# A hybrid attention and conv-GLU layer on one core: first loads in another order and partly from ScalarE, and two output-projection tiles side by side

## Chip, cores and metric

One core of a Trainium2 chip runs the kernel. The metric is the device time of one execution in microseconds. Three runs of the kernel before gave 912.3, 916.3 and 916.69 us, median 916.3.

## What is computed

One layer over 16 meta tokens and 512 tokens of width 1024 (528 rows in all): three kinds of attention, gated and merged, an output projection, and a feed-forward part with a convolution of width 3. All of it is float32.

```python
u = rmsnorm(h, attn_norm)
z = u @ w_in                     # q, k, v of three branches, the indexer's q, k, w, three gates
y_sb = stick_breaking(...)       # 4 heads
y_sp = indexed_sparse(...)       # 4 heads, top 132 keys by the indexer's score, relative bias
y_df = differential(...)         # 4 heads with two softmaxes each, relative bias
merged = sum(sigmoid(g + b) * (y @ w_br))      # over the three branches
h = h + merged @ w_out
u = rmsnorm(h, ffn_norm)
gate, val = split(u @ w_up)
h = h + (silu(conv3(gate) + conv_b) * val) @ w_down
return h[16:528]
```

## The kernel before

Everything is held transposed: 128 channels on the partitions, tokens along the free dimension. The weights come as 133 chunks of 128 x 1024 float32 (512 KB each), every chunk the eight 128 x 128 tiles of one output tile. A product is made of three matmuls: both operands are split into a high part that TensorE takes in one pass and a low part, and the three products high-high, high-low and low-high are added up in PSUM (`mm3`, lines 311 to 324). So each chunk needs a cast on ACT (`wh`, line 306) and a subtraction (`wl`, line 307) that goes to DVE or POOL by booked costs (`sub`). There are three buffers for raw chunks, and two each for `wh` and `wl`. `order` (line 279) lists the chunks as they are used; `prep` loads two chunks ahead, from the SP queue.

An engine's instructions run in the order in which they were recorded. A layer of the kernel records them with a small model of the engines' clocks (`Timed`, `pe`, `tick`), and the tile framework may move an instruction by priority; what comes out is fixed before the kernel runs.

**The start (lines 339 to 415).** `prm` is a table of parameters, its first 40 columns are the gains. `hT` comes in eight k-tiles `hs[0..7]` (264 KB each, named `tmp<-hT`). Two chunks, W_IX (chunk 0) and W_QIX (chunk 1), are loaded in halves of four tiles (256 KB). Line 386 loops over the k-tiles: ACT scales one into `xh`, DVE makes `xl`, ACT squares it, and PE makes 12 matmuls, six for W_IX into `psw` and six for W_QIX into `psd`. After the last, DVE's sum of squares goes through a matmul with `onesd` (line 413), and `rstd` makes the reciprocal root on ACT and DVE; the results in PSUM are multiplied by it when they leave. Chunk 2 is W_QIX's second tile, chunks 3 and on are the attention units' q, k and v.

**The bias table.** `bias` (97 rows of 664 numbers) is loaded into `braw` by POOL at line 439. `bias_stream` (line 441) is a side stream: ACT casts parts of `braw` into two tiles `brd`, DVE makes a low part, and later a matmul and DMAs spread the table out. PE's matmul on `brd` comes at 39 us.

**The output projection (lines 1058 to 1099).** `mh` and `ml` are the split of the merged branches, eight k-tiles. Tile m uses chunk 59 + m: two halves of the tokens (258 and 256), 24 matmuls each, into one bank `psd` and one `psw` that `psx` hands out in turn. The first tile goes k-tile by k-tile in groups (0 to 3), (4, 5), (6), (7), since the last k-tiles of `mh` and `ml` come late. Then DVE adds the result to `hm`, ACT makes `uh` and the squares, DVE `ul`, POOL sums the squares.

In the profile nearly all work of DVE, ACT and POOL stands at line 99 (the helper that books it), and matmuls at line 183; so one goes by the tiles' names.

Of the kernel before, what the change touches and what calls it, by code (L numbers as in the profile page):

```python
# [15 lines left out]
P = 128  # L16
# [18 lines left out]
C_AN, C_FN, C_BG, C_QSP, C_KSP, C_QDF, C_KDF, C_SUB, C_CB, C_CW, C_LAM = (  # L35
    0, 8, 16, 40, 41, 42, 43, 44, 45, 67, 133)
# [3 lines left out]
W_IX, W_QIX, W_UNIT, W_GATE = 0, 1, 3, 27  # L40
# [15 lines left out]
def tile_kernel(ctx: ExitStack, tc, hT, wpk, par, bias, yT):  # L56
    nc = tc.nc
# [83 lines left out]
    def psd():  # L141
        return ps.tile([P, 512], F32, tag="d", bufs=banks["d"], name="psd")
# [36 lines left out]
    def mm(out, lhsT, rhs, **k):  # L179

        n, w = rhs.shape[-1], 0.84 * max(32, lhsT.shape[-1])
        pe(max(0.46 * n + 1, w) if rhs.dtype == F32R else 2 * max(0.844 * n, w))
        PE.matmul(out, lhsT, rhs, **k)  # L183
# [11 lines left out]
    def tick():  # L195
        for s in list(streams):
            cur[0] = s[1]
            try:
                next(s[0])
            except StopIteration:  # L200
                streams.remove(s)
        cur[0] = main
# [35 lines left out]
            n += 1  # L238
            assert n < 10000, (free, clock)

    nc.scalar.preload_act_table_set("natural_log_exp_and_others")


    prm = const.tile([P, NPAR], F32, name="prm")

    def pc(c):
        return prm[:, c:c + 1]
# [29 lines left out]
    wraw, wsp = {}, {}  # L277
    plan = PLAN.split()
    order = [W_IX, W_QIX, W_QIX + 1]
    for w in plan:  # L280
# [5 lines left out]
        else:  # L286
            n = BRW[br] // 2
# [5 lines left out]
    def load(k):  # L293
        if k is not None and k not in wraw:
            r = wp.tile([P, 8, P], F32, tag="raw", bufs=3, name=f"wr{k}")
            nc.sync.dma_start(r, wpk[k].rearrange("p (j c) -> p j c", c=P))
            wraw[k] = r

    def prep(k):
        if k is None or k in wsp:  # L300
            return
        load(k)
        r = wraw[k]
        wh = wp.tile([P, 8, P], F32R, tag="wh", bufs=2, name=f"wh{k}")
        wl = wp.tile([P, 8, P], F32R, tag="wl", bufs=2, name=f"wl{k}")
        S.copy(wh, r)
        sub(wl, r, wh, HVW)
        wsp[k] = (wh, wl)
        load(after.get(after.get(k)))

    def mm3(out, prs, xh, xl, start=True, stop=True):

        n = len(prs)
        c = 0
        for pas in range(3):
            for e, (k, j, kt) in enumerate(prs):
                wh, wl = wsp[k]
                w = wl if pas == 2 else wh
                x = xl if pas == 1 else xh
                mm(out, w[:, j, :], x(kt), start=start and pas == 0 and e == 0,  # L320
                   stop=stop and pas == 2 and e == n - 1)
                c += 1
                if c % 8 == 0:
                    tick()

    HALF = ((0, TH), (TH, TH))
    HALQ = ((0, HQ), (HQ, 256))
# [11 lines left out]
    def load_h(*kts):  # L339
        for kt in kts:  # L340
            nc.sync.dma_start(hs[kt], hT[:, kt])

    def load_half(k, a):
        nc.sync.dma_start(wraw[k][:, a:a + 4], wpk[k].rearrange("p (j c) -> p j c", c=P)[:, a:a + 4])


    nc.sync.dma_start(prm[:, :C_QSP], par[:, :C_QSP])
    load_h(0)
    load_half(W_IX, 0)
    load_half(W_QIX, 0)  # L350
    load_h(1, 2)
    load_half(W_IX, 4)
    load_h(3)
    load_half(W_QIX, 4)
    load_h(4, 5)
    nc.sync.dma_start(prm[:, C_QSP:], par[:, C_QSP:])
    load_h(6, 7)
    load(order[2])

    def wbank():  # L360
        return ps.tile([P, 512], F32, tag="w", bufs=banks["w"], name="psw")
# [16 lines left out]
    def psx():  # L378
        flip[0] ^= 1
        return psd() if flip[0] else wbank()  # L380
# [55 lines left out]
    tab = dram.tile([8, NREL], F32, name="tab")  # L436
    gd = [dram.tile([P, NREL], F32, name=f"gd{h}") for h in range(8)]
    braw = ap_.tile([97, 4, TQ], F32, tag="G", bufs=4, name="braw").rearrange("p a b -> p (a b)")[:, :8 + NREL]
    nc.gpsimd.dma_start(braw, bias)

    def bias_stream():
        yield from wait("qk", 2)
# [615 lines left out]
    mh = xp.tile([P, KT, TQ], F32R, tag="xh", name="mh")  # L1058
    ml = xp.tile([P, KT, TQ], F32R, tag="xl", name="ml")
    for m in range(8):  # L1060
        a = gates[0, m // 4][:, m % 4]
# [12 lines left out]
    def ft(dt=F32):  # L1074
        return ffn.tile([P, TQ], dt, tag="ft", bufs=10, name="ft")

    for m in range(8):
        nc.sync.dma_start(hm[:, m], hT[:, m, Q0:])
        k = W_OUT + m
        prep(k)  # L1080
        prep(after.get(k))
        ds = [psx(), psx()]
        for js in ((0, 1, 2, 3), (4, 5), (6,), (7,)) if m == 0 else ():

            for (o, n), d in zip(HALQ, ds):
                mm3(d[:, :n], [(k, j, j) for j in js], lambda kt: mh[:, kt, o:o + n],
                    lambda kt: ml[:, kt, o:o + n], start=js[0] == 0, stop=js[0] == 7)
        for (o, n), d in zip(HALQ, ds):
            if m:
                mm3(d[:, :n], [(k, j, j) for j in range(KT)], lambda kt: mh[:, kt, o:o + n],  # L1090
                    lambda kt: ml[:, kt, o:o + n])
            V.tensor_tensor(hm[:, m, o:o + n], hm[:, m, o:o + n], d[:, :n], OP.add)
        g = pc(C_FN + m)
        S.activation(uh[:, m], hm[:, m], AF.Copy, scale=g)
        V.scalar_tensor_tensor(ul[:, m], hm[:, m], g, uh[:, m], OP.mult, OP.subtract)
        sq = ss if m == 0 else ft()
        S.activation(sq, hm[:, m], AF.Square)
        if m:
            G.tensor_tensor(ss, ss, sq, OP.add)
# [33 lines left out]
    for f in range(NF):  # L1133
# [6 lines left out]
        c = ft()  # L1140
# [4 lines left out]
        a = ft()  # L1145
# [9 lines left out]
    for m in range(8):  # L1155
        y = ft()
        d = psd()
        e0, e1 = m * NF, (m + 1) * NF
        for c in sorted({e // 8 for e in range(e0, e1)}):
            k = W_DN + c  # L1160
# [4 lines left out]
                start=es[0] == e0, stop=es[-1] == e1 - 1)  # L1165
# [77 lines left out]
```

## Time and profile before

| | us |
|---|---|
| three runs | 912.3, 916.3, 916.69 |
| median | 916.3 |
| the profiled execution, its own time | 915.66 |
| its span, first to last instruction | 913.9 |
| PE busy | 872.8 |
| DVE busy | 546.3 |
| ACT busy | 453.6 |
| POOL busy | 324.4 |

The span is what the trace shows; the 1.8 us between it and the execution's own time lie around it. The profiled execution is 0.64 us under the median. The mean granted clock of TensorE over the span is 0.992.

### The profile page before, as it was taken

What the parts mean: (1) busy time and instruction counts of PE and PEld (TensorE: products, weight loads), DVE (VectorE), ACT (ScalarE), POOL (GpSimd) and SP (SyncE); (2) the same over time, 40 slices, a digit from 0 to 9 for tenths busy, and PEclk for the clock granted to TensorE, in tenths of its full rate; (3) what the DMA queues carried; (4) which work ended last, traced back from release to release, by engine and by line L of the source; (5) the groups of instructions that cost most, each with busy time, mean ns of one, the idle gap of its engine ahead of it and who ended that gap; (6) DMA issues with size and microseconds to landing.
All of it is one profiled execution on the core that took longest, in us unless ns stands there. A gap on an engine that the chain in (4) does not pass through costs nothing.

```text
span 913.9 us, 15423 instructions
## 1 busy us (share of the span) xinstructions
PE 872.8 (96%) x6066; PEld 809.5 (89%) x6066; DVE 546.3 (60%) x1125; ACT 453.6 (50%) x848; POOL 324.4 (36%) x195
## 2 busy tenths in 40 slices
PE   6998989899999999879998999999999999999998
PEld 6988988889999999779998999999999999888886
DVE  6579999997564765787437445555555555422221
ACT  6566785677846787734744344333333333211110
POOL 1433334243255424666354233333334444200100
PEclk9999999999999999999999999999999999999999
DMA  6586212433234423332233423333333233333330
GB/s 231 159 229 197 70 47 64 105 96 105 64 93 129 129 81 88 100 94 71 70 92 110 146 77 105 96 94 93 93 93 93 93 93 93 93 116 106 114 102 23
DMA packets 32359, 94.68 MB, mean 104 GB/s; under 512 B 4313, under 2 KB 4457, under 8 KB 32288
## 3 DMA queue, kind: packets, MB, share of 16 engines
q1 hardware_dynamic: 31568, 91.30, 34.0%
q0 software_dynamic: 720, 2.42, 1.0%
q8 instruction: 47, 0.77, 0.4%
q14 instruction: 24, 0.20, 0.1%
HBM read 80.88 MB, written 5.86 MB: 95 GB/s over the span
## 4 chain that ended last, share of the span: by engine, by line
PE 74%; DVE 17%; ACT 3%; DMA 2%; issue 2%; POOL 1%; SPq 0%; DVEq 0%; ACTq 0%; POOLq 0%
PE psd L183 51%; PE psw L183 21%; DVE tmp L99 6%; DVE work L99 4%; DVE m L99 2%; DMA qk<-qk 1%; PE psw L187 1%; ACT tmp L99 1%; DVE G L99 1%; DMA wr<-wpk 1%; DVE pt L99 1%; POOL wl L99 1%; ACT wh L99 0%; ACT G L99 0%; DVE ml L99 0%
## 5 line engine op out<-in xcount | busy, mean ns | idle before, releaser
L99 POOL TENSOR_TENSOR wl<-wr,wh 128x1024 fp32r<-128x1024 f32 x79 | 194.6, 2463 | 345.3 <-ACT wh L99 256.9
L99 ACT CAST wh<-wr 128x1024 fp32r<-128x1024 f32 (+2 forms) x137 | 139.6, 1021 | 174.0 <-PE psd L183 118.5
L183 PE MATMUL psd<-xh,wh 128*128 128x258 f32 (+2 forms) x792 | 118.6, 290 | 3.0 <-ACT wh L99 2.1
L183 PE MATMUL psd<-xl,wh 128*128 128x258 f32 (+2 forms) x792 | 119.3, 291 | 0.0
L183 PE MATMUL psd<-xh,wl 128*128 128x258 f32 (+2 forms) x792 | 117.4, 288 | 0.0
L99 DVE TENSOR_TENSOR wl<-wr,wh 128x1024 fp32r<-128x1024 f32 (+3 forms) x58 | 67.0, 1157 | 70.6 <-PE psd L183 60.6
L183 PEld LDWEIGHTS psd<-xh,wh 128*128 128x128 f32 x792 | 104.4, 191 | 4.5 <-ACT wh L99 2.4
L183 PEld LDWEIGHTS psd<-xl,wh 128*128 128x128 f32 x792 | 105.5, 191 | 1.1
L183 PEld LDWEIGHTS psd<-xh,wl 128*128 128x128 f32 x792 | 104.3, 190 | 0.7
L99 ACT ACTIVATE tmp<-tmp 128x264 f32<-128x264 f32 (+7 forms) x154 | 69.1, 475 | 28.5 <-DVE tmp L99 26.5
L99 POOL TENSOR_TENSOR ft<-ft 128x512 f32<-128x512 f32 x22 | 46.8, 2128 | 81.9 <-DVE ft L99 78.5
L99 DVE SCALAR_TENSOR_TENSOR ft<-ft,prm 128x512 f32<-128x512 f32 x44 | 58.5, 1329 | 20.4 <-ACT ft L99 19.6
L183 PE MATMUL psw<-uh,wh 128*128 128x256 f32 (+2 forms) x264 | 47.0, 320 | 0.0
L183 PE MATMUL psd<-ul,wh 128*128 128x258 f32 (+2 forms) x264 | 46.9, 319 | 0.0
L183 PE MATMUL psw<-ul,wh 128*128 128x256 f32 (+2 forms) x264 | 46.9, 319 | 0.0
L183 PE MATMUL psd<-uh,wl 128*128 128x258 f32 (+2 forms) x264 | 46.8, 319 | 0.0
L183 PE MATMUL psw<-uh,wl 128*128 128x256 f32 (+2 forms) x264 | 46.8, 319 | 0.0
L183 PE MATMUL psd<-uh,wh 128*128 128x258 f32 (+2 forms) x264 | 46.8, 319 | 0.0
L183 PE MATMUL psd<-al,wh 128*128 128x512 f32 x176 | 45.8, 396 | 0.0
L183 PE MATMUL psd<-ah,wl 128*128 128x512 f32 x176 | 45.8, 396 | 0.0
L183 PE MATMUL psd<-ah,wh 128*128 128x512 f32 x176 | 45.8, 396 | 0.0
L99 ACT CAST ah<-ft 128x512 fp32r<-128x512 f32 x22 | 13.7, 621 | 64.3 <-POOL ft L99 64.3
(193 smaller groups left out, 1642.6 us busy)
## 6 DMA issues: line engine op xcount, KB each, us to landing
wr<-wpk SPq DMA_DIRECT2D x131, 512.0 KB, 3.6
qk<-qk SPq DMA_DIRECT2D x48, 132.0 KB, 3.4
gd<-tab SPq DMA_DIRECT2D x8, 328.0 KB, 6.7
tmp<-hT SPq DMA_DIRECT2D x8, 264.0 KB, 6.8
W<-gd POOLq DMA_DIRECT2D x8, 264.0 KB, 3.4
qk<-tmp SPq DMA_DIRECT2D x16, 128.5 KB, 2.7
hm<-hT SPq DMA_DIRECT2D x8, 257.0 KB, 5.2
yT<-ft SPq DMA_DIRECT2D x8, 256.0 KB, 2.0
```

The costliest lines, as they stand in the source:

```text
L99: return f(out, *a, **k)
L183: PE.matmul(out, lhsT, rhs, **k)
L187: PE.transpose(out, x, ident[:x.shape[0], :x.shape[0]])
```

## The change

The two chunks' first halves and the gains go out first, two of the three from ACT's own queue: `prm` and the half of W_QIX on ACT, the half of W_IX on SP. ACT's table load comes after these issues. Then SP issues the k-tiles and the second halves in another order. The bias table is loaded by SP where POOL did it. In the output projection the first two tiles are recorded together, for k-tiles (0 to 4), (5), (6), (7).

```diff
-    nc.scalar.preload_act_table_set("natural_log_exp_and_others")
...
-    def load_half(k, a):
-        nc.sync.dma_start(wraw[k][:, a:a + 4], wpk[k].rearrange("p (j c) -> p j c", c=P)[:, a:a + 4])
-
-
-    nc.sync.dma_start(prm[:, :C_QSP], par[:, :C_QSP])
-    load_h(0)
+    def load_half(k, a, q=nc.sync):
+        q.dma_start(wraw[k][:, a:a + 4], wpk[k].rearrange("p (j c) -> p j c", c=P)[:, a:a + 4])
+
+
+    nc.scalar.dma_start(prm[:, :C_QSP], par[:, :C_QSP])
     load_half(W_IX, 0)
-    load_half(W_QIX, 0)
-    load_h(1, 2)
+    load_half(W_QIX, 0, nc.scalar)
+    nc.scalar.preload_act_table_set("natural_log_exp_and_others")
+    load_h(0, 1, 2)
     load_half(W_IX, 4)
     load_h(3)
     load_half(W_QIX, 4)
-    load_h(4, 5)
+    load_h(4, 5, 6, 7)
     nc.sync.dma_start(prm[:, C_QSP:], par[:, C_QSP:])
-    load_h(6, 7)
     load(order[2])
...
-    nc.gpsimd.dma_start(braw, bias)
+
+    nc.sync.dma_start(braw, bias)
...
-        ds = [psx(), psx()]
-        for js in ((0, 1, 2, 3), (4, 5), (6,), (7,)) if m == 0 else ():
-
-            for (o, n), d in zip(HALQ, ds):
-                mm3(d[:, :n], [(k, j, j) for j in js], lambda kt: mh[:, kt, o:o + n],
-                    lambda kt: ml[:, kt, o:o + n], start=js[0] == 0, stop=js[0] == 7)
+        if m == 0:
+
+            both = [[psx(), psx()] for _ in range(2)]
+            for js in (range(0, 5), (5,), (6,), (7,)):
+                for a, ds in enumerate(both):
+                    for (o, n), d in zip(HALQ, ds):
+                        mm3(d[:, :n], [(k + a, j, j) for j in js], lambda kt: mh[:, kt, o:o + n],
+                            lambda kt: ml[:, kt, o:o + n], start=js[0] == 0, stop=js[0] == 7)
+        ds = both[m] if m < 2 else [psx(), psx()]
         for (o, n), d in zip(HALQ, ds):
-            if m:
+            if m > 1:
                 mm3(d[:, :n], [(k, j, j) for j in range(KT)], lambda kt: mh[:, kt, o:o + n],
```

What comes out of the recording, at the three places that matter.

SP's first instructions before (`wr_104` is W_IX, `wr_107` W_QIX, `wr_132`, `wr_279` and `wr_345` chunks 2, 3 and 4):

```order
L347 DMA prm<-par 128x40
L341 DMA tmp<-hT 128x528
L344 DMA wr_104<-wpk 128x512
L344 DMA wr_107<-wpk 128x512
L341 DMA tmp<-hT 128x528 x2
L344 DMA wr_104<-wpk 128x512
L341 DMA tmp<-hT 128x528
L344 DMA wr_107<-wpk 128x512
L341 DMA tmp<-hT 128x528 x2
L356 DMA prm<-par 128x349
L341 DMA tmp<-hT 128x528 x2
L296 DMA wr_132<-wpk 128x1024
```

and of the change (W_IX is `wr_103` now, W_QIX `wr_106`):

```order
L342 DMA wr_103<-wpk 128x512
L339 DMA tmp<-hT 128x528 x3
L342 DMA wr_103<-wpk 128x512
L339 DMA tmp<-hT 128x528
L342 DMA wr_106<-wpk 128x512
L339 DMA tmp<-hT 128x528 x4
L354 DMA prm<-par 128x349
L294 DMA wr_132<-wpk 128x1024
L294 DMA wr_279<-wpk 128x1024
L437 DMA braw<-bias 97x664
L294 DMA wr_345<-wpk 128x1024
```

The gains and the half of W_QIX are gone to ACT, and the bias table stands between chunks 3 and 4; the load of chunk 3 has to wait until DVE has read all of W_IX, whose raw buffer it takes.

ACT at the end of the start before (`tmp<-tmp` are squares, `wh_341` chunk 2, `wh_364` chunk 3, `rs` and the two rows behind it `rstd`):

```order
L99 ACTIVATE xh<-tmp,prm 128x528
L99 ACTIVATE tmp<-tmp 128x528
L99 CAST brd<-braw 97x328
L99 CAST brd<-braw 97x8
L99 ACTIVATE tmp<-tmp 128x528
L99 CAST brd<-braw 97x328
L99 CAST wh_341<-wr_132 128x1024
L99 CAST wh_364<-wr_279 128x1024
L99 ACTIVATE rs<-psw,eps 128x264 x2
```

and of the change:

```order
L99 ACTIVATE tmp<-tmp 128x528 x3
L99 CAST brd<-braw 97x8
L99 CAST brd<-braw 97x328
L99 CAST brd<-braw 97x8
L99 CAST brd<-braw 97x328
L99 CAST wh_341<-wr_132 128x1024
L99 ACTIVATE lam<-lam 128x2
L99 CAST wh_364<-wr_279 128x1024
L99 ACTIVATE rs<-psw,eps 128x264 x2
```

All four casts of the bias table now stand together behind the last square and ahead of chunk 2's cast, and `lam` has moved ahead of chunk 3's.

PE where the first output tile ends, before (`wh_6468` and `wl_6469` are chunk 59, `wh_6570` and `wl_6571` chunk 60, `wh_6632` chunk 61):

```order
L183 MATMUL psw<-mh,wh_6468 128x256
L183 MATMUL psw<-ml,wh_6468 128x256
L183 MATMUL psw<-mh,wl_6469 128x256
L183 MATMUL psd<-mh,wh_6570 128x258
L183 MATMUL psd<-ml,wh_6570 128x258 x8
L183 MATMUL psd<-mh,wl_6571 128x258 x8
L183 MATMUL psw<-mh,wh_6570 128x256 x3
L183 MATMUL psw<-ml,wh_6570 128x256 x8
L183 MATMUL psw<-mh,wl_6571 128x256 x8
L183 MATMUL psd<-mh,wh_6632 128x258 x8
```

and of the change (chunk 61 is `wh_6682`):

```order
L183 MATMUL psw<-mh,wh_6468 128x256
L183 MATMUL psw<-ml,wh_6468 128x256
L183 MATMUL psw<-mh,wl_6469 128x256
L183 MATMUL psd<-mh,wh_6570 128x258
L183 MATMUL psd<-ml,wh_6570 128x258
L183 MATMUL psd<-mh,wl_6571 128x258
L183 MATMUL psw<-mh,wh_6570 128x256
L183 MATMUL psw<-ml,wh_6570 128x256
L183 MATMUL psw<-mh,wl_6571 128x256
L183 MATMUL psd<-mh,wh_6682 128x258 x8
```

Between the last matmul on chunk 59's `wh` and the first on chunk 61's, which takes the same buffer, stood 37 matmuls; now there are seven. The recording had put 12 matmuls of the second tile into the first one's gaps before; that is 10 now, ahead of the same wait.

## Rows read from the trace of the kernel before

**Rows 1.** The page's line of busy time, share and instructions of each engine.

```profile
PE 872.8 (96%) x6066; PEld 809.5 (89%) x6066; DVE 546.3 (60%) x1125; ACT 453.6 (50%) x848; POOL 324.4 (36%) x195
```

**Rows 2.** Waits of PE, whole span: total us, times, longest us.

```profile
PE psw L183 <- ACT wh L99: 5.4, 1, 5.4
...
PE psd L183 <- DVE ml L99: 2.6, 2, 1.9
PE psd L183 <- ACT wh L99: 2.1, 1, 2.1
```

**Rows 3.** Timeline of PE: start, us, instructions, in brackets idle time before and releaser.

```profile
5.37 0.81 PE L183 MATMUL psw<-xh,wh 128*128 128x264 f32 x2 [5.37 <-ACT wh L99]
9.34 0.79 PE L183 MATMUL psd<-xh,wh 128*128 128x258 f32 x2 [2.11 <-ACT wh L99]
...
22.75 1.05 PE L183 MATMUL psw<-tmp,onesd 128*128 128x264 f32 x4
...
37.33 1.13 PE L183 MATMUL psd<-xh,wh 128*128 128x264 f32 x8
```

**Rows 4.** Chain of waits up to 31 us: start, us, what.

```profile
2.13 6.83 DMA wr<-wpk
...
22.94 1.04 ACT wh L99
...
30.43 0.59 PE psd L183 x3
```

**Rows 5.** Busy time by stretch: length, PE, PEld, DVE, ACT, POOL, granted clock, DMA, GB/s.

```profile
9.30:14.60 5.30, 5.26 (x23) 5.18 (x24) 4.97 (x9) 5.30 (x10) 0.00 (x0) 1.00 1.06 399
14.60:18.00 3.40, 3.40 (x30) 3.40 (x29) 3.40 (x6) 3.40 (x8) 0.00 (x0) 1.00 0.93 326
```

**Rows 6.** The output projection: timeline of PE, then two stretches as in rows 5.

```profile
486.45 0.39 PE L183 MATMUL psd<-ml,wh 128*128 128x258 f32 x1 [0.70 <-DVE ml L99]
...
491.71 0.39 PE L183 MATMUL psd<-ml,wh 128*128 128x258 f32 x1 [1.93 <-DVE ml L99]
...
489.10:492.50 3.40, 1.47 (x12) 1.27 (x12) 3.40 (x4) 0.62 (x1) 1.40 (x1) 1.00 0.27 52
492.50:495.90 3.40, 3.40 (x18) 3.40 (x17) 1.57 (x3) 0.00 (x0) 0.00 (x0) 0.51 0.45 142
```

**Rows 7.** Timeline of DVE and POOL ahead of the late `ml`.

```profile
487.58 2.92 POOL L99 TENSOR_TENSOR wl<-wr,wh 128x1024 fp32r<-128x1024 f32 x1 [1.74 <-ACT wh L99]
...
488.19 2.86 DVE L99 TENSOR_TENSOR G<-G,G 128x514 f32<-128x514 f32 x1
```

**Rows 8.** ACT up to 26 us, by shape: count, busy us, mean ns, idle before.

```profile
L99 ACT ACTIVATE xh<-tmp,prm 128x528 fp32r<-128x528 f32 x8 | 5.6, 730 | 2.4 <-DMA tmp<-hT 2.4
L99 ACT ACTIVATE tmp<-tmp 128x528 f32<-128x528 f32 x8 | 4.9, 639 | 0.4 <-DVE xl L99 0.4
...
L99 ACT CAST brd<-braw 97x328 fp32r<-97x328 f32 x2 | 0.9, 452 | 0.0
L99 ACT CAST brd<-braw 97x8 fp32r<-97x8 f32 x2 | 0.4, 187 | 0.0
```

**Rows 9.** DMA from 4.7 to 8.3: POOL's queue (packets, MB, share); the table's issue (KB, us).

```profile
q0 software_dynamic: 80, 0.26, 24.3%
...
braw<-bias POOLq DMA_DIRECT2D x1, 251.6 KB, 6.6
```

**Rows 10.** Timeline of DVE: the second half of W_IX's low part.

```profile
11.74 0.69 DVE L99 TENSOR_TENSOR wl<-wr,wh 128x512 fp32r<-128x512 f32 x1
```

**Rows 11.** Timeline of PE, ACT and POOL: chunk 59's release and chunk 61.

```profile
497.16 0.28 PE L183 MATMUL psw<-ml,wh 128*128 128x256 f32 x1
...
497.52 1.05 ACT L99 CAST wh<-wr 128x1024 fp32r<-128x1024 f32 x1 [5.82 <-PE psw L183]
498.65 2.40 POOL L99 TENSOR_TENSOR wl<-wr,wh 128x1024 fp32r<-128x1024 f32 x1 [8.15 <-ACT wh L99]
...
501.75 1.13 PE L183 MATMUL psd<-mh,wh 128*128 128x258 f32 x8
```

## The prediction

> **What bounds the kernel now.** I read the page's busy shares first, then the waits of PE, then the timelines of the two places that the change touches. PE is busy for 872.8 us, 96% of the span [rows 1], so this is a PE-bound kernel, and what an edit is worth is read from the idle and slow time of PE beside it. The list of waits names two such places [rows 2]: at the start PE waits for ACT's `wh` for 5.4 us and again for 2.1, and later it waits for DVE's `ml` for 2.6. The reader should see that these are 10 of PE's some 41 idle us; what else it waits for lies in parts that the change leaves alone.
>
> The first 31 us: matmuls begin at 5.37, stop after 7.2, and go on at 9.34, when the first half of W_QIX has landed and been cast [rows 3]; the chain of waits puts that load at 6.83 us, from 2.13 to 8.97 [rows 4]. Up to 14.6 PE gets through 23 recorded matmuls in 5.3 us, after it 30 in 3.4 us [rows 5]: 0.23 us each against 0.11 (records are missing, so somewhat less in both), so it works at the lower of its two levels (1.2 GHz) until it has been busy for 5.3 us without a gap. The column of the granted clock reads 1.00 there, and only the spacing shows it. From 22.94 the chain is no longer matmuls: ACT casts chunk 2, then come ACT's and DVE's reciprocal root and PE's next free bank at 30.43 [rows 4].
>
> The output projection: PE stops for 0.70 and 1.93 us for `ml`, and from 492.5 to 495.9 it is granted 0.51 of its clock after it was busy for only 1.47 of the 3.4 us before [rows 6]. The late part is DVE's: its add `G<-G,G` takes 2.86 us while POOL works on a `wl` [rows 7].
>
> **The change, part by part.** *The first loads.* PE's first matmul now needs both first halves, `prm` and h0 (256 + 256 + 264 + 20 KB) where it needed 540. The 256 more cost 0.65 us at the 399 GB/s of that stretch [rows 5]; W_IX goes out first, two issues earlier than before. So the first matmul comes between 5.0 and 6.0; I take 5.5. The table load, 1.3 us long, moves behind two issues on ACT and is hidden: ACT waits 2.4 us for h0 anyway [rows 8]. The wait at 7.2 goes. If PE then works without a gap, and rises after 5.3 us as now, some 25 matmuls take it to 10.8 and the other 71 of 96, at 0.12 each, to 19.3, with the statistics' matmuls 0.35 behind the last k-tile at 19.65; before, these began at 22.75 [rows 3]. ACT has to keep up: its scalings and squares (5.6 + 4.9 us [rows 8]) and the casts of two chunks (2.1 us by the 1.04 of one [rows 4]), some overlapped, from 4.8 on end at about 17, early enough. So 3.1 us are to be had, at most 3.4, and nothing if something on ACT is late.
>
> *What is late next.* The bias table `braw`, 97 rows, was loaded by POOL at 2.34; it now stands on SP behind the load of chunk 3. ACT's four `brd` casts wait for it, and they stand in ACT's order ahead of the cast of chunk 2 (`wh_341`), of `lam`, chunk 3 and all of `rstd`; DVE's `brd`, `lam` and second part of `rstd` stand behind them too, and POOL's `wl`. Before, three of these casts fell into gaps of ACT between 15.4 and 19.7, and the table had been there for long: 6.6 us from issue to landing [rows 9].
>
> When does it land? Chunk 3 is issued when DVE has made W_IX's second `wl`: at 12.43 before [rows 10]. Counted through ACT and DVE in the new order, about 11.4, so `braw` is issued near 12. The 524 kB of chunk 3 stand in front and take 1.3 us, so it begins at about 13.7. Then it depends on how many of the 16 DMA engines carry it, which no row shows: all SP transfers of the trace have 128, 64, 32 or 8 rows (the order and the names' shapes tell this). The near bound is the full rate, 258 kB at 399 GB/s, 0.65 us: landing before 15, no wait. The far bound is one engine: 399/16 = 24.9 GB/s, 10.4 us, landing at 24.1; or, taken from POOL's own transfer, 24.3% of 16 engines for 3.6 us, 14.0 us of engine time in a crowd [rows 9], landing at 27.7. 97 has no even share but one engine for all, and an SP transfer with uneven shares is not in the trace, so I take one engine, alone on an otherwise quiet queue: 24.1.
>
> The Trainium skill, "DMA: Bandwidth & Descriptors", section "Why a DMA increments its semaphore by 16 and not by 1", has a rule that speaks against this edit: a transfer issued from SP or ACT is spread over the largest number of engines, up to 16, that divides its row count on both sides, while GpSimd's may be shared unevenly. For 97 rows that is one engine. By it the sum is the one below; without it, that of the first rival. No run so far shows an SP load of 97 rows.
>
> From 24.1: casts 2 x (0.19 + 0.45), overlapped to 1.1 us, then `wh_341` in 1.0 [rows 8, 4]: 26.2, where it ended at 22.94 before, as chunk 3's cast began [rows 4]. That is 3.3 us later, after PE stood idle for some 6 us, and all that follows in the chain keeps its distance. PE comes back at the lower level, but until 30.43 it has 7.4 us for 48 matmuls, which need 5.8 at the upper and 8.1 if the rise takes 5.3 us; I add 0.3. Chunk 4's share on that one engine lands near 25.5 and is not needed before 37.33 [rows 3]. The first part costs **+3.6 us**, with bounds -3.4 and +7.5 (landing at 27.7 and the full 8.1).
>
> *The output projection.* Of its first 96 matmuls 26 stand ahead of the one that waits for `ml` of the fourth k-tile (491.71), in both orders, and 70 behind it; DVE, ACT and POOL keep their order up to there. So neither the waits nor the end (501.75) move, and the part is worth nothing there. What moves is the release of chunk 59's buffers. The cast of chunk 61 waits for them: it began 0.36 us after the start of the last matmul on `wh_6468` (497.16), took 1.05, POOL's `wl` took 2.40 more [rows 11], and 37 matmuls, nearly all of tile 1, covered both. Now seven matmuls (0.84 us) stand between. The cast is ready 1.46 us after that matmul and PE could go on after 0.96: 0.5 us of waiting. The low part is ready 2.5 us later still, while 16 matmuls need 1.92: 0.6 more. Behind the cast on ACT stand `uh`, the squares and chunk 62's cast, which have 5.8 us of matmuls as cover. **+1.1 us**; bounds 0 and +1.6 (POOL at the 2.92 of [rows 7]). The stretch at the lower level costs 1.7 us (3.4 at 0.51); it may or may not come again, so -1.7 belongs to the range.
>
> POOL loses one issue and SP three; neither is on the chain. `hm` loads move ahead of chunk 64's, first used three tiles later. Both cost nothing.
>
> **Sum.** The profiled execution took 915.66 us (span 913.9), 0.64 under the median of 916.3. 915.66 + 3.6 + 1.1 = **920.4**.
>
> **The rivals.** *The rows are shared.* `braw` then lands before 15, ACT is free at about 18, and PE's early end holds: -3.1, and the stall at the third tile stays, +1.1: 913.7. For it: POOL's transfer of the same rows took 80 packets in 3.6 us, beside others. Against it: no uneven share on SP. Chance 0.17. *The engine is slower, on the slow side.* At 14.0 us the table lands at 27.7, PE begins chunk 2 near 29.8 after 9 us of idling and runs 25 matmuls at the lower level: 915.66 + 7.5 + 1.1 = 924.3. It decides from a landing after 25.5. For it: POOL's transfer paid just this; against: it ran beside the loads, and the queue is quiet after 15. Chance 0.16. *The projection does what it is written for:* the idle time falls so that the lower level is not granted, and the buffers come in time: 915.66 + 3.6 - 1.7 = 917.6. Against it: 26 matmuls on either side. Chance 0.13. That the start gains nothing at all because ACT's issues delay its casts would hide under the table's wait and changes no sum.
>
> **How the numbers follow.** The forecast has 0.50; 0.04 is left for others. A measurement of this kernel can tell about 0.5%: below 911.7 or above 920.9. The forecast's 920.4 lies just inside; with +-2 us for its own terms, 0.22 of its 0.50 is above. With 0.16 of the slow engine and 0.02 of the rest: slower 0.40. Shared rows lie within the bound for 0.11 and below it for 0.06, with 0.01 of the rest: faster 0.07. The others: 0.53. The range goes from 912.5 (shared rows, part of the lower level gone) to 925.5 (slow engine, its bound). The forecast's own range is 918 to 923.
>
> **What would show it.** Right: no wait at 7.2 and matmuls at 0.12 us from about 11; `braw` with more than 10 us to landing; PE idle from 20 to 26 with ACT waiting for that DMA; two waits of about 0.6 us for `wh` and `wl` where the third tile begins. Wrong: `braw` landing within 3 us, ACT without a wait at the `brd` casts, chunk 2's matmuls at 20; or tile 1's end earlier than 16.7 us after the first matmul on `mh`.

## The result, and the profile after

The kernel with the change takes 924.2 us (median of six runs, 923.08 to 924.99), the kernel before beside it 916.5: a ratio of 1.0089, 95% interval 1.0073 to 1.0106. The profiled execution took 924.43 us with a span of 922.0; the span is 8.1 us longer than before. The forecast was 920.4, 0.45% over the kernel before; the kernel came out 0.89% over the one beside it. 924.2 lies inside the wide range (912.5 to 925.5) and above the forecast's own (918 to 923).

PE's busy time has hardly moved [rows 1]:

```profile
PE 875.1 (95%) x6066; PEld 811.8 (88%) x6066; DVE 550.1 (60%) x1125; ACT 453.4 (49%) x848; POOL 323.4 (35%) x194
```

The list of PE's waits (total us, times, longest us), against [rows 2], tells where to look: the two waits for the halves of the first chunks have become one of 7.0 for the first `xh`, a new one of 7.3 for `wh` stands at the head, the wait for `ml` is unchanged, and there is one for POOL's `wl`.

```profile
PE psd L183 <- ACT wh L99: 7.6, 2, 7.3
PE psw L183 <- ACT xh L99: 7.0, 1, 7.0
...
PE psd L183 <- DVE ml L99: 2.8, 3, 1.9
...
PE psd L183 <- POOL wl L99: 0.3, 1, 0.3
```

The timeline of PE at the start (against [rows 3]):

```profile
6.97 0.81 PE L183 MATMUL psw<-xh,wh 128*128 128x264 f32 x2 [6.97 <-ACT xh L99]
...
10.67 0.40 PE L183 MATMUL psw<-xh,wl 128*128 128x264 f32 x2
...
20.32 1.05 PE L183 MATMUL psw<-tmp,onesd 128*128 128x264 f32 x4
28.66 2.09 PE L183 MATMUL psd<-xh,wh 128*128 128x258 f32 x8 [7.28 <-ACT wh L99]
...
37.01 1.11 PE L183 MATMUL psd<-xh,wh 128*128 128x258 f32 x8
...
43.84 1.13 PE L183 MATMUL psd<-xh,wh 128*128 128x264 f32 x8
```

The eight k-tiles are done at 20.32 where it was 22.75. Little of that is idle time saved (6.97 us now, 5.37 and 2.11 before); most is that the matmuls leave the lower clock at 10.67 and not at 14.6. Then PE stands for 7.28 us until chunk 2 has been cast, and its first eight matmuls take 2.09 us where eight at 37.01 take 1.11: it comes back at the lower clock. ACT tells why, with SP's issue of the table ahead of it:

```profile
12.84 0.33 SPq L437 DMA_DIRECT2D braw<-bias  x1
```

```profile
5.98 0.30 ACT L99 CAST wh<-wr 128x128 fp32r<-128x128 f32 x1 [1.69 <-DMA wr<-wpk]
...
17.71 0.65 ACT L99 ACTIVATE tmp<-tmp 128x528 f32<-128x528 f32 x1 [0.65 <-DVE xl L99]
26.63 1.03 ACT L99 CAST brd<-braw 97x8 fp32r<-97x8 f32 x4 [8.28 <-DMA braw<-bias]
27.57 1.04 ACT L99 CAST wh<-wr 128x1024 fp32r<-128x1024 f32 x1
```

ACT has nothing left to do at 18.36 but the table's casts, waits 8.28 us for the table, and only then casts chunk 2. Its casts begin 13.8 us after the table's issue. (The wait of 1.69 us at the top is that for the half of W_QIX; it comes up again below.) What the DMA did meanwhile stands in the busy times by stretch (columns as in [rows 5]; the last three are granted clock, DMA share, GB/s):

```profile
22.00:24.00 2.00, 0.00 (x0) 0.00 (x0) 0.00 (x0) 0.00 (x0) 0.00 (x0) 1.00 0.07 27
24.00:26.00 2.00, 0.00 (x0) 0.00 (x0) 0.00 (x0) 0.00 (x0) 0.00 (x0) 0.54 0.06 25
```

No engine works, the DMA is busy for 0.06 of its 16 engines, which is one of them, and moves 25 to 27 GB/s. In the trace the table's 97 row packets run one after another from 15.36 to 26.16 (the first expectation names both 0.45 us too late). The granted clock falls in the second stretch, after PE has stood since 21.4.

The output projection on PE (against [rows 6] and [rows 11]):

```profile
492.12 0.75 PE L183 MATMUL psd<-mh,wh 128*128 128x258 f32 x5
...
498.82 0.58 PE L183 MATMUL psd<-ml,wh 128*128 128x258 f32 x1 [1.91 <-DVE ml L99]
...
509.24 1.23 PE L183 MATMUL psd<-mh,wh 128*128 128x258 f32 x8 [0.34 <-ACT wh L99]
...
511.72 1.23 PE L183 MATMUL psd<-mh,wl 128*128 128x258 f32 x8 [0.30 <-POOL wl L99]
...
515.67 1.13 PE L183 MATMUL psd<-mh,wh 128*128 128x258 f32 x8
```

The wait for the last `ml` is as long as it was (1.91 against 1.93), and two new ones stand where the third tile begins. So the 8.1 us can be laid out by the same matmul in both traces:

| PE begins | before | after | later by |
|---|---|---|---|
| the statistics (`onesd`) | 22.75 | 20.32 | -2.43 |
| chunk 2 | 23.44 | 28.66 | 5.22 |
| chunk 3 | 30.43 | 37.01 | 6.58 |
| chunk 4 | 37.33 | 43.84 | 6.51 |
| the projection's first matmul on `mh` | 485.00 | 492.12 | 7.12 |
| the third tile | 501.75 | 509.24 | 7.49 |
| the fourth tile | 507.50 | 515.67 | 8.17 |
| the end of the span | 913.9 | 922.0 | 8.1 |

The start costs 6.5 us, the projection 1.05, and 0.6 come in between.

### The profile page after: what moved, and what is told of

Same layout as the page of the kernel before. It is cut to its first block, busy times and chain, and to the rows that moved or that the text cites. A ratio compares the mean times of both kernels' runs of the same rounds, so it can differ in the third digit from the quotient of the medians.

```text
span 922.0 us, 15426 instructions
## 1 busy us (share of the span) xinstructions
PE 875.1 (95%) x6066; PEld 811.8 (88%) x6066; DVE 550.1 (60%) x1125; ACT 453.4 (49%) x848; POOL 323.4 (35%) x194
## 5 line engine op out<-in xcount | busy, mean ns | idle before, releaser
L99 ACT CAST ah<-ft 128x512 fp32r<-128x512 f32 x22 | 13.7, 621 | 64.6 <-POOL ft L99 64.6
```

The lines of the kernel that those rows point to most:

```text
L99: return f(out, *a, **k)
```

## The experiments

The theory: one DMA engine carries the table's 97 rows, and what costs is that its casts stand ahead of chunk 2's on ACT. The rivals: the loads that ACT issues are to blame; SP's queue or the place in it is; the projection is. The comparisons are with the kernel before, run on the same chip beside each.

### The table from POOL again

```diff
-    nc.sync.dma_start(braw, bias)
+    nc.gpsimd.dma_start(braw, bias)
```

> The change, but the bias table loaded by POOL as before. Theory (ACT's brd casts, and behind them chunk 2's cast, wait for a table that one DMA engine carries from 15.8 to 26.6): the table lands before 10 us, ACT has no wait at the brd casts, PE begins chunk 2 at 21 to 22 (28.66 with the change, 23.44 before), and the time is 914 to 916.5: 1.2 to 2.4 us won at the start, 1.05 lost in the output projection. First rival (the loads issued by ACT are what costs: PE's first matmul came at 6.97 instead of 5.37): chunk 2 begins at 24 or later and the time stays above 920. Second rival (the projection costs most of the 7.7 us): above 922.

Measured: 916.77 us, ratio 1.0014 (1.0005 to 1.0024). PE's timeline and the table's row among the DMA issues (KB, us to landing):

```profile
21.19 1.30 PE L183 MATMUL psd<-xh,wh 128*128 128x258 f32 x8
```

```profile
braw<-bias POOLq DMA_DIRECT2D x1, 251.6 KB, 7.0
```

Chunk 2 begins at 21.19, and by the ratios 0.75% of the loss of 0.89% is gone. The loads from ACT are not what costs, and neither is the projection for its greater part. The time is 0.3 us above the range expected, and its ratio is that of the new projection alone (1.0014, below): in the time, the 2.25 us won at the start don't show. In the profile they are lost again between chunk 4 and the projection (35.02 to 485.35, 450.3 us, against 447.7 before); the trace's clock record has the lower level for 20.5 us of that stretch, against 10.2 before. More on this in the last section.

### The table in two loads, 96 rows and one

```diff
-    nc.sync.dma_start(braw, bias)
+    nc.sync.dma_start(braw[:96], bias[:96])
+    nc.sync.dma_start(braw[96:97], bias[96:97])
```

> The change, but the table still from SP in the same place as two loads, of 96 rows and of one. Theory (97 rows in one load go to one engine, 96 can be shared evenly by 16): both land within 3 us of their issue, before 17; ACT waits less than 0.5 us at the brd casts; PE begins chunk 2 near 21.0; 914 to 916. Rival (SP's queue or the place behind chunk 3 is what is late, whatever the rows): the landing stays beyond 24, chunk 2 begins after 26, and the time is 921 to 925.

Measured: 915.27 us, ratio 1.0004 (0.9994 to 1.0015). The load of 96 rows among the DMA issues, and ACT:

```profile
braw<-bias SPq DMA_DIRECT2D x1, 249.0 KB, 4.4
```

```profile
18.18 0.18 ACT L99 CAST brd<-braw 97x8 fp32r<-97x8 f32 x1
19.55 1.05 ACT L99 CAST wh<-wr 128x1024 fp32r<-128x1024 f32 x1 [1.20 <-PE psw L183]
...
23.54 0.92 ACT L99 CAST brd<-braw 97x328 fp32r<-97x328 f32 x3
```

But for the last row, the same bytes on the same queue in the same place land in 4.4 us (under 3 was expected). ACT has no wait at the casts, and PE begins chunk 2 at 21.01. The edit changed the recorded order too: only one of the four casts stands ahead of chunk 2's now. That one reads all 97 rows and did not wait, so the table was there by 18.18, in time for all four. That rules out the rival that SP's queue or the place is late: it is the count of rows in one load.

### The kernel before, with the table from SP

```diff
-    nc.gpsimd.dma_start(braw, bias)
+    nc.sync.dma_start(braw, bias)
```

> The kernel before with one edit: the table loaded by SP behind chunk 3. The brd casts now stand behind rstd in ACT's order, not ahead of chunk 2's cast. Theory (the slow transfer costs only through what stands behind the casts on ACT): it lands between 24 and 27 again, more than 10 us after its issue, chunk 2 still begins within 0.3 us of 23.4, ACT waits up to 1.5 us at the casts, and the time is 916 to 917.5. Rival (the long transfer on one engine costs by itself, by holding up the chunks' loads that share the engine): chunks 3 to 5 are late, PE waits for them, and the time is 919 or more.

Measured: 915.14 us, ratio 1.0002 (0.999 to 1.0014). PE and ACT:

```profile
20.98 1.30 PE L183 MATMUL psd<-xh,wh 128*128 128x258 f32 x8
...
28.33 1.20 PE L183 MATMUL psd<-xh,wh 128*128 128x258 f32 x8 [1.16 <-DVE tmp L99]
```

```profile
25.40 1.03 ACT L99 CAST brd<-braw 97x8 fp32r<-97x8 f32 x4 [1.79 <-DMA braw<-bias]
```

The slow load is here too: issued at 10.79, awaited until 25.40. But its casts stand behind `rstd`, ACT waits 1.79 us for them, and the kernel isn't slower; 916 to 917.5 was expected. The expectation missed one thing: chunk 2 begins at 20.98, not at 23.4. With the table off POOL's queue the first loads come sooner, PE's stop after 7.2 us is gone, and the statistics begin at 20.29. So the gain at the start that the change's order of loads brings is to be had without that order. In this profile (913.4 us) chunk 4 is 2.0 us ahead of before (35.30 against 37.33); the median doesn't show that gain.

### The change, with chunk 4 ahead of the table

```diff
+    load(order[4])
     nc.sync.dma_start(braw, bias)
```

> The change with one edit: chunk 4 is loaded ahead of the table, which stays one SP load of 97 rows. In ACT's order the brd casts now stand behind the casts of chunks 2 and 3 and behind rstd. Theory (it is not the slow load that costs, but what stands behind its casts): the table lands even later, at 27 to 30, and still PE begins chunk 2 at 20.8 to 21.3 with no wait of 7 us; ACT waits 3 to 6 us at the casts, which delays what follows by up to 3 us and PE by up to 1.5; 915 to 917.5. Rival (a load of 97 rows from SP costs by itself, wherever its casts stand): 920 or more.

Measured: 920.08 us, ratio 1.0039 (1.0025 to 1.0053). By the time alone the rival is right. PE and ACT:

```profile
20.70 1.30 PE L183 MATMUL psd<-xh,wh 128*128 128x258 f32 x8
...
31.34 2.06 PE L183 MATMUL psd<-xh,wh 128*128 128x258 f32 x8 [4.46 <-DVE tmp L99]
```

```profile
28.94 1.03 ACT L99 CAST brd<-braw 97x8 fp32r<-97x8 f32 x4 [5.61 <-DMA braw<-bias]
29.87 0.41 ACT L99 CAST tmp<-tmp 96x264 fp32r<-96x264 f32 x1
```

```profile
29.17 0.16 DVE L99 TENSOR_TENSOR brd<-braw,brd 33x8 fp32r<-33x8 f32 x1 [3.06 <-ACT brd L99]
...
30.77 0.43 DVE L99 TENSOR_TENSOR tmp<-psd,rs 128x258 f32<-128x258 f32 x1
```

Chunk 2 begins at 20.70, as the theory has it, and the table lands at about 28.9. My price for what stands behind the casts there was too low, and it missed an engine: DVE's own small `brd` work stands in DVE's order ahead of the `tmp<-psd,rs` that empties PE's next bank. With the table in two loads it took its turn at 26.46 and waited for nothing; here DVE stands 3.06 us for ACT's cast, the bank comes free after 30.77, PE stands 4.46 us at chunk 3, and comes back at the lower clock. (The cast of `tmp` 96x264 behind the casts on ACT is late too, 29.87 for 26.46, but DVE shows no wait for it.) So, against the kernel before, the same load cost nothing, 4 us or 8 us by what stands behind its readers on ACT and DVE: 25.40 was early enough for that, 28.94 was not. The first of the three is the least sure: against its own kernel with the table in two loads (last experiment, 0.9975) it is 2.5 us longer by the ratios, with intervals that just touch, though PE begins chunk 4 no later (35.30 against 35.66).

### The new projection alone, in the kernel before

The change's last part, as in its diff.

> The kernel before with the change's output projection alone. Theory (two new waits at the third tile, 0.34 and 0.30 us with the change, and no gain ahead of them, since 26 matmuls stand ahead of the late ml in both orders): 0.6 to 1.4 us more, 917.1 to 917.9, with the two waits in the trace. Rival (side by side the two tiles fill the waits for ml, or the stretch at the lower clock goes): 914 to 916. A third possibility, nothing beyond noise: 916.2 to 917.

Measured: 916.45 us, ratio 1.0014 (1.0003 to 1.0025), 1.3 us by the ratio and inside the 0.6 to 1.4 expected; the kernel before took 915.53 beside it, so the time itself is under the 917.1 named. PE:

```profile
502.01 1.23 PE L183 MATMUL psd<-mh,wh 128*128 128x258 f32 x8 [0.34 <-ACT wh L99]
...
504.49 1.23 PE L183 MATMUL psd<-mh,wl 128*128 128x258 f32 x8 [0.30 <-POOL wl L99]
```

The two waits are there without the rest of the change. From the first matmul on `mh` to the fourth tile PE needs 23.64 us (484.79 to 508.43), 22.50 before.

### The table in two loads, with the old projection

The edit of the second experiment, and the old projection's lines put back.

> The change with the table in two loads (96 rows and one) and the output projection of before: what is left is the new order of the first loads and the table on SP. Theory (the new projection costs two waits at the third tile, 0.64 us in all, and 0.4 ahead of them): 0.6 to 1.3 us under the same kernel with the new projection (915.27), that is 914.0 to 914.7, 0.1 to 0.2% faster than before; no wait for wh or wl at the third tile. Rival (the projection is worth nothing either way): 915 to 915.6.

Measured: 914.68 us, ratio 0.9981 (0.9967 to 0.9994), 0.2% under the same kernel with the new projection (1.0004). No wait for `wh` or `wl` is left at the third tile. In this execution the lower clock was not granted at the projection either:

```profile
491.00:494.40 3.40, 3.40 (x28) 3.40 (x29) 2.30 (x4) 0.00 (x0) 0.00 (x0) 1.00 0.43 148
```

Its projection takes 20.99 us to the fourth tile (484.25 to 505.24), 1.51 less than before, near what [rows 6] gave as the price of that stretch (1.7). So this profile doesn't part the two waits from the clock.

### Side by side, but the first tile ends first

```diff
-            for js in (range(0, 5), (5,), (6,), (7,)):
-                for a, ds in enumerate(both):
-                    for (o, n), d in zip(HALQ, ds):
+            seq = [(range(0, 5), 0), (range(0, 5), 1)] + [((j,), a) for a in range(2) for j in (5, 6, 7)]
+            for js, a in seq:
+                if 1:
+                    for (o, n), d in zip(HALQ, both[a]):
```

with the table in two loads.

> The change with the table in two loads, and the new projection in another order: both tiles for k-tiles 0 to 4, then k-tiles 5 to 7 of the first tile, then 5 to 7 of the second. Now 19 matmuls stand between the last on chunk 59's wh and the first on chunk 61's, not seven. Theory (the wait at the third tile is the short cover of chunk 61's cast and low part): both waits, 0.34 and 0.30 us, are gone or under 0.1, the time is 0.4 to 0.9 us under that of the kernel with the table in two loads (915.27): 914.4 to 914.9. Rival (the waits come from ACT or POOL being late for another reason): they stay, 915.0 to 915.6.

Measured: 914.39 us, ratio 0.997 (0.9955 to 0.9986), the lowest ratio of all. PE at the third and fourth tile:

```profile
501.03 1.12 PE L183 MATMUL psd<-mh,wh 128*128 128x258 f32 x8
...
506.77 1.13 PE L183 MATMUL psd<-mh,wh 128*128 128x258 f32 x8
```

Both waits are gone, and with them 1.34 us from the first matmul on `mh` to the fourth tile (22.31 against 23.65 with the table in two loads), 0.68 of it between the third and the fourth (5.74 against 6.42). So it was the cover of seven matmuls. The wait for `ml` is 1.91 still: side by side the tiles win next to nothing over one after the other (22.31 against 22.50 before, both with a stretch at the lower clock).

### Loads with other counts of rows

Five loads of 2 KB rows in the output projection, beside the table in two loads:

```diff
+        r = {2: 96, 3: 95, 4: 98, 5: 74, 6: 97}.get(m)
+        if r:
+            t = ffn.tile([P, TQ], F32, tag="ft", bufs=10, name=f"rows{r}")
+            nc.sync.dma_start(t[:r, :512], hT[:r, m, :512])
+            nc.gpsimd.tensor_copy(t[:r, 512:513], t[:r, :1])
```

> The change with the table in two loads, and five more loads of 2 KB rows from SP in the output projection (96, 95, 98, 74 and 97 rows, one for each of tiles 2 to 6, each read by one small POOL copy; their data is not used). Theory (an SP load is shared by the largest number of engines up to 16 that divides its rows, at the 25 GB/s that one engine moved for the table): 96 rows by 16 engines, 98 by 14, 95 by 5, 74 by 2, 97 by 1, so 0.5, 0.6, 1.6, 3.0 and 8.0 us of transfer beside a constant of 2 to 5 us: landing times in the order 96, 98, 95, 74, 97, with 97 more than 5 us above 96 and 74 some 2.5 above. Rival (97 was slow because of where it stood, not its count): all five within 1.5 us of each other. A third possibility, only odd counts are slow: 74 and 98 like 96. The time itself tells nothing here.

Each stands behind a chunk's load on the queue, and POOL's copies of 95, 98 and 74 rows found them landed, so the landing times tell only that 97 is the slowest: issued at 526.0, awaited by POOL until 537.57, where 96 rows came 4.3 us after their issue.

```profile
537.57 0.19 POOL L1106 COPY rows<-rows 97x1 f32<-97x1 f32 x1 [4.45 <-DMA rows<-hT]
```

The expected order of the landing times is not shown that way. By the trace's packets the transfers took 1.4 us (96 rows), 1.4 (98), 2.1 (95), 3.2 (74) and 8.0 (97): the theory's order, but for 96 and 98, which are level. The third possibility, that only odd counts are slow, falls with the 74 rows. The number of engines can be read from the last two columns of single us in which nothing else is to be seen, for 95, 74 and 97 rows (for 96 and 98 no such us stands alone):

```profile
513.00:514.00 1.00, 1.00 (x11) 1.00 (x10) 1.00 (x2) 1.00 (x2) 0.00 (x0) 1.00 0.32 125
...
524.00:525.00 1.00, 1.00 (x10) 1.00 (x9) 1.00 (x2) 0.69 (x2) 0.00 (x0) 1.00 0.13 51
...
529.00:530.00 1.00, 1.00 (x10) 1.00 (x10) 0.26 (x1) 0.89 (x1) 0.00 (x0) 1.00 0.06 25
```

0.32, 0.13 and 0.06 of 16 engines are five, two and one, at 125, 51 and 25 GB/s, 25 for each. The 97 rows' packets run from 528.98 to 536.99, 8.0 us as expected.

### The kernel before with the table in two loads, and with the better tile order too

The first has the one edit of the table; the second the projection of the run where the first tile ends first as well. Both keep the old order of the first loads.

> The kernel before with one edit: the table from SP behind chunk 3 in two loads (96 rows and one). First loads and projection as before. Theory (what the start gains in the runs with the table repaired comes from taking the table out of the first loads' way, not from the loads issued by ACT and their order): PE begins chunk 2 at 20.7 to 21.3, as with the new order of loads (21.0), ACT has no wait at the brd casts, and the time is 0.1 to 0.3% under before: 913.8 to 915.5, within 0.7 us of the kernel with the new loads, the table in two and the old projection. Rival (the new order of the first loads is what gains): chunk 2 at 22.3 or later, and no gain over before.

> The kernel before with the table in two loads from SP and the projection in which the first tile ends first; first loads as before. Theory: no wait for wh or wl at the third tile, chunk 2 at 20.7 to 21.3, and a time like that of the same projection with the new loads (ratio to before 0.997): 913 to 915. If the new order of loads has a worth of its own, this is 0.5 us or more above that; if it costs, below.

Measured: 914.01 us, ratio 0.9975 (0.9958 to 0.9992), and 914.82 us, 0.9982 (0.9966 to 0.9997). Chunk 2 begins at 21.42 and 19.91 (20.7 to 21.3 was expected of both), beside 21.33 and 21.97 in the two kernels with the new loads. In the first of the two PE's early stop is short, and in the second it is gone:

```profile
7.71 0.80 PE L183 MATMUL psd<-xh,wh 128*128 128x258 f32 x2 [0.76 <-ACT wh L99]
```

So once the table is off POOL's queue, the order of the first loads and their issue from ACT have no worth that these runs show. With the table on POOL's queue the order does bring chunk 2 forward (21.19 against 23.44, first experiment), though not the time. The intervals of the four kernels (0.9981, 0.997, 0.9975, 0.9982) overlap, and which is fastest stays open. All four beat the change, and the kernel before by 0.2 to 0.3%, with intervals that end just under 1.

## Where the prediction was right, and where it failed

*The mechanism of the start* was right. The wait at 7.2 goes, the table takes one engine, and PE stands from 21 on behind ACT's casts. The runs show each link: the count of rows (96 and one), and the order on ACT (three places, three prices); the loads from ACT are not what PE waits for at chunk 2. That the matmuls reach 0.12 us apart at about 11 (0.24 for two from 10.67 on) came out by luck: they began 1.5 us later than forecast and left the lower clock after 3.7 us, not 5.3.

*The size of the start* was too small: 3.6 forecast, 6.5 measured. The step that failed is the landing at 24.1, and in it the begin of the transfer at 13.7; ACT went on at 26.63. Of the 2.5 us missing, 0.85 are the issue (12.84, not 12.0), as W_IX's second `wl` ended a us later than counted; 0.8 the wait behind chunk 3 (first packet 15.36, not 13.7, so 2.5 us after the issue and not 1.7); 0.4 the transfer (10.8 against 10.4), and 0.5 the way from the last packet to ACT. I had let chunk 3 run at the full rate from its issue on. By their order, its packets run from 13.43 to 15.35, after those of chunk 2 (11.24 to 13.43), which stands ahead of it on the queue and which the sum left out.

*The lower clock* was the second term too small: 0.3 forecast. Chunk 2's cast ended 5.7 us later than before (28.61 against 22.94), chunk 3's matmuls began 6.6 later, so PE's return at the lower level cost 0.9. (At 22.94 in [rows 4] stands the cast of chunk 3; the prediction's first reading calls it chunk 2's, its sum has it right.)

*The first matmul* came at 6.97, not at 5.5, because ACT waited for the half of W_QIX that it had issued itself (1.69 us, until 5.98). The prediction said that such a delay would hide under the table's wait and change no sum. PE's part of it did hide; but ACT, which works without idle time from 5.98 on, casts W_IX's second half the later for it, and so DVE's `wl`, chunk 3 and the table's issue are late: these are the 0.85 above. With the old order of loads the table was issued at 10.79 and its packets began at 14.50. In the repaired kernels the start gains 2.4 us (chunk 2 at 21.01) where 3.1 was counted; that the late first matmul is what holds it is not shown, as chunk 2 began at 20.98 where the first matmul came at 5.42 (third experiment).

*The projection* was right in its place, cause and size: 1.1 forecast, 1.05 measured, 26 matmuls ahead of the late `ml` in both orders, and the two waits for `wh` and `wl`. The waits are 0.34 and 0.30 us in the rows where 0.5 and 0.6 were expected, but each cost PE more than its idle time (last section). SP loses two issues and gains one, where the prediction counts three lost; nothing hangs on that.

*The rival of the slow engine* named 924.3, but not for its reason. Its 14.0 us of engine time were 10.8. Its other half, that everything hangs on a landing after 25.5, was what happened, by a late begin. So the range held the time, and the chances did not lean the right way: "same", within 0.5% of before, had 0.53 with a forecast that stood 0.5 us from that bound (920.9). The bounds of the landing reached from 15 to 27.7, and between the forecast and its upper end I had asked only for the rate of the engine and not for the begin.

The Trainium skill, "DMA: Bandwidth & Descriptors", section "Why a DMA increments its semaphore by 16 and not by 1", gives for a load from SP the largest number of engines up to 16 that divides the rows. The rows agree for 97, 95 and 74: one, five and two engines.

## What to carry to other kernels

Before a load is moved to SP's or ACT's queue, count its rows: 97 rows in one load went through one DMA engine at 25 GB/s and took 10.8 us, and of the same table in two loads the 96 rows were there 4.4 us after their issue. What a late load cost was set by what stood behind its readers in their engines' orders: against the kernel before nothing, 4 us or 8 us. And when two tiles are computed side by side, the buffers of both come free close to the end of the last one: end one of them first, so that the next chunk's cast has cover.

## What the runs showed of the hardware

A wait of PE cost more than its row. When both waits at the third tile went, the stretch from there to the fourth fell by 0.68 us, though only the 0.30 for `wl` lie in it: 0.43 at that wait, and 0.12 and 0.11 in the groups of matmuls that come right after the two waits. The row counts from the modelled end of the last matmul, and matmuls that follow each other overlap: the one at 508.62 lasts 0.28 and the next would have begun 0.12 after it; it began 0.62 after it, so the 0.34 us for `wh` cost 0.50.

The time between the start and the projection is not fixed. The kernels with the table in two loads, without and with the loads of other row counts, are the same program up to the projection. From chunk 2 to the first matmul on `mh` one execution took 462.87 us (21.01 to 483.88), the other 461.62 (21.39 to 483.01). That is why 1 us at the start is hard to find again in a single run's time. Part of it goes with the granted clock: from chunk 4 to the projection the lower level stood for 20.5 us in the first and for 13.7 in the second, for 10.2 in the kernel before, 13.7 with the change and 20.5 with the table from POOL. It is not all: 447.7 us went with 10.2 at the lower level, 447.5 with 13.7 (the kernel before with the table from SP), 448.8 and 450.3 with 20.5. So it may hold the 0.6 us of the change and the 2.7 lost with the table from POOL, but that is not shown. At the projection the lower clock was granted in the profile of before and of the change, and not in the two with the old projection and the table in two loads. What decides this wasn't tried.
